# Attention's meta-value product as one fp32r product over 128 stacked rows, and the halo queries' output as one product

## The chip, the cores and the metric

The kernel runs on one core of one Trainium2 chip. The metric is the device time of one execution in microseconds, median of three runs: 1804.35 us before (1803.9 to 1806.26). A profile comes from one further execution, which took 1806.76 us itself; its span from the first to the last instruction is 1805.0 us.

## The reference, cut to what matters

Two hybrid blocks run one after the other over 512 tokens of width 1024. The first has an SSD branch, a sliding-window attention branch and a feed-forward part; the second has other mixers. The change touches only the attention of the first block. There, 16 query heads share two key/value heads of width 64. Every query of a block of 128 tokens sees the previous and its own block, and beside them 16 meta tokens that stand ahead of the sequence; a sink value joins the softmax.

```
s = concat(s_meta, s_band, sink)          # 16 + 256 + 1 columns per query
p = softmax(s)
p_meta = p[..., :16];  p_band = p[..., 16:-1]
out = einsum(p_meta, v_meta) + einsum(p_band, v_band)
```

The first of the two products of the last line, `p_meta` with `v_meta`, is what the change is about. All of it is fp32.

## The kernel before, in words

Activations lie with channels on the 128 partitions and tokens along the free axis. A weight matrix is loaded in tiles of 128x1024 (`wload`, line 67), and each tile is cut into a high part in fp32r (ScalarE copy, line 76) and the low rest (VectorE subtraction, line 77). A projection (`gemm`, lines 88 to 90) then makes three fp32r products for each 128x128 weight: high with high, high with low, low with high. A product whose operands are plain fp32 runs as two passes in the profile (two LDWEIGHTS and two MATMUL records for each call).

Attention (line 508) works on pairs of heads: `j` runs from 0 to 7, and in each pair the head of the first key/value head lies on partitions 0 to 63 and that of the second on 64 to 127. Its setup makes `kh` and `kl` (keys, high and low), `vtok` (values with tokens on the partitions), and `vm`: the 16 meta values of both key/value heads as a block-diagonal matrix of 32 rows and 128 columns (transpose at line 550, copy at line 551). Two halo queries ahead of the sequence see only meta tokens; lines 554 to 583 make their softmax and their output, the latter by eight small products of `vm` with two columns of `pth` each (line 581).

`scores(j)` (line 585) makes the scores of pair `j`, adds the bias, and takes the softmax in `s`. `values(j, s)` (line 627) makes the output:

```
pm = psum(g)                                            # four transposes: 32 meta columns x 512 queries (L633)
nc.vector.tensor_copy(ptm, pm[:32, :])                  # L634
pv = psum(g, "o")
nc.tensor.matmul(pv, vm, ptm, start=True, stop=False)   # L637
```

Then, for each of four query blocks, the band columns of `s` are transposed (lines 646 and 650), copied by ScalarE to `pt` (647, 651) and multiplied with `vtok` (656, 657) into the same accumulation `pv`. The product at line 637 opens this accumulation, so the 14 products (28 passes) of lines 656 and 657 of a pair stand behind it. ScalarE copies `pv` back over the queries (658).

The loop calls `scores(j + 1)` ahead of `values(j)`, and after each pair `fill` (line 226) adds two or three gate or branch projections (`gate_tile`, line 669, and `branch`, line 470), which are plain `gemm` work. PSUM has three buffers with the tag "g" (projections), two "a" (scores), two "t" (transposes; `pm` and the halo's are of these) and one "o" (`pv`).

The order in which each engine gets its instructions is not that of the program text. A planner goes over the whole program with priorities in the order of the text (weight loads come ahead, `high_priority`), simulates the engines with its own costs, and writes down a fixed order for every engine. In the trace, transposes, scores, projections and value products of several steps alternate on TensorE. An engine then executes its order strictly, waiting where it must.

When the attention's tiles are released, the tiles `ah` and `al` (line 58 and 59 of `split_hl`) take their place: the attention output cut into high and low parts, on which the next projection works. So the last pair's output stands ahead of everything that follows.

Of the kernel before, what the change touches and what calls it, by code (L numbers as in the profile page):

```python
# [12 lines left out]
F32 = mybir.dt.float32  # L13
F32R = mybir.dt.float32r
# [3 lines left out]
AF = mybir.ActivationFunctionType  # L18
ALU = mybir.AluOpType
# [96 lines left out]
def psum(g, tag="t"):  # L116
    return g.pp.tile([128, 512], F32, name=f"ps_{tag}", tag=tag, bufs=g.psb[tag])
# [90 lines left out]
LINE = 64  # L208
# [9 lines left out]
class Mixer:  # L218
# [289 lines left out]
    def attention(self, wk, nfill):  # L508
        g, nc = self.g, self.nc
# [18 lines left out]
        for k in range(2):  # L528
            r, z = half[k], half[1 - k]
# [18 lines left out]
        vm = wk.tile([32, 128], F32, name="vm", tag="vm")  # L548
        px = psum(g)
        nc.tensor.transpose(px[:32, :128], vbd, g.ident)  # L550
        nc.scalar.activation(vm, px[:32, :128], AF.Copy)
        sink = g.par[:, _BP["sink"]:_BP["sink"] + 16]

        hb = wk.tile([2, 256], F32, name="hb", tag="hb")
        nc.sync.dma_start(out=hb, in_=g.a["bias_h"])
        ph = psum(g)
# [17 lines left out]
        ph = psum(g)  # L574
        for j in range(8):
            nc.tensor.transpose(ph[:32, j * 2:j * 2 + 2], sh[:, j * 32:(j + 1) * 32], g.ident[:2, :2])
        pth = wk.tile([32, 16], F32, name="pth", tag="pth")
        nc.vector.tensor_copy(pth, ph[:32, :16])
        ph = psum(g)
        for j in range(8):  # L580
            nc.tensor.matmul(ph[:, j * 2:j * 2 + 2], vm, pth[:, j * 2:j * 2 + 2], start=True, stop=True)
        halo = wk.tile([128, 16], F32, name="halo", tag="halo")
        nc.vector.tensor_copy(halo, ph[:, :16])

# [41 lines left out]

        def values(j, s):
            q = qs[j]
            ptm = wk.tile([32, 512], F32, name="ptm", tag="ptm", bufs=2)
            pm = psum(g)  # L630
            for b in range(4):
                m0 = 256 if b else 128
                nc.tensor.transpose(pm[:32, b * 128:(b + 1) * 128], s[:, b, m0:m0 + 32], g.ident)  # L633
            nc.vector.tensor_copy(ptm, pm[:32, :])  # L634

            pv = psum(g, "o")
            nc.tensor.matmul(pv, vm, ptm, start=True, stop=False)  # L637
            for b in range(4):
                pt = wk.tile([128, 2, 2, 128], F32, name="pt", tag="pt", bufs=3)
                ptf = pt.rearrange("p a b c -> p (a b c)")  # L640
                px = psum(g)
                if b:
                    for k in range(2):
                        for t in range(2):
                            c0 = k * 288 + t * 128
                            nc.tensor.transpose(px[:, (k * 2 + t) * 128:(k * 2 + t + 1) * 128], s[:, b, c0:c0 + 128], g.ident)  # L646
                    nc.scalar.activation(ptf, px, AF.Copy)
                else:
                    for k in range(2):
                        nc.tensor.transpose(px[:, k * 128:(k + 1) * 128], s[:, 0, k * 160:k * 160 + 128], g.ident)  # L650
                    nc.scalar.activation(pt[:, :, 1, :], px[:, :256].rearrange("p (a c) -> p a c", a=2), AF.Copy)
                cols = slice(b * 128, (b + 1) * 128)
                for k in range(2):
                    rows = slice(k * 64, k * 64 + 64)
                    if b:
                        nc.tensor.matmul(pv[rows, cols], vtok[:, b - 1, rows], pt[:, k, 0, :], start=False, stop=False)
                    nc.tensor.matmul(pv[rows, cols], vtok[:, b, rows], pt[:, k, 1, :], start=False, stop=(b == 3))
            nc.scalar.activation(q[:, 2:NO], pv, AF.Copy)
            nc.vector.tensor_copy(q[:, 0:2], halo[:, 2 * j:2 * j + 2])

        prev = scores(0)
        for j in range(8):
            nxt = scores(j + 1) if j < 7 else None
            values(j, prev)
            prev = nxt
            self.fill(nfill[j])
# [905 lines left out]
```

## Time and profile before

| | before |
|---|---|
| median of 3 runs | 1804.35 us |
| profiled execution | 1806.76 us |
| its span | 1805.0 us |
| TensorE busy (matmul) | 1761.6 us, 98% |
| VectorE busy | 1135.6 us, 63% |
| ScalarE busy | 753.4 us, 42% |
| GpSimd busy | 296.2 us, 16% |
| mean granted TensorE clock | 0.992 |

"Busy" of TensorE counts from a pass's start to its modelled end, and passes overlap; so the share alone does not tell how much could be saved, and the distance between the starts of two passes is the better measure of what one costs. Line numbers (L637) are those of the kernel before; a line of a helper stands for all its callers, and the tile names tell them apart.

### The profile page before, as it was taken

To read this page: it belongs to the slowest core of one execution; us is meant where nothing else is said; L and a number is where in the kernel's file an instruction comes from. 1 tells how busy PE (TensorE), PEld (TensorE's weight loads), DVE (VectorE), ACT (ScalarE), POOL (GpSimd) and SP (SyncE) were. 2 spreads that over 40 slices of the span, in tenths; PEclk is the share of its full clock that TensorE was granted. 3 is DMA by queue.
4 is the path that set the end of the run, shared out by engine and by line. 5 is a ranking of instruction groups with operands and counts; after the bars stand their busy time and mean duration, and the time that the engine had idled before them with its cause. 6 is when DMAs were issued, how large, how long until landed. Compare 5 with 4: busy or idle time off the path is not lost.

```text
span 1805.0 us, 29863 instructions
## 1 busy us (share of the span) xinstructions
PE 1761.6 (98%) x12108; PEld 1590.8 (88%) x12108; DVE 1135.6 (63%) x2151; ACT 753.4 (42%) x1334; POOL 296.2 (16%) x287
## 2 busy tenths in 40 slices
PE   8999999999999999999999999999999999999997
PEld 8999999999889889999999988878888777878887
DVE  7797787855586755466677533577665676743543
ACT  4544444432336553334444433564443345632233
POOL 1254444533330002200000011100000000000112
PEclk9999999999999999999999999999999999999999
DMA  4223222222222222222222222221222121222222
GB/s 153 98 90 106 88 96 83 95 94 95 87 75 76 75 94 94 94 82 95 94 94 92 91 97 96 83 91 62 82 71 91 65 72 43 87 84 93 94 94 71
DMA packets 51341, 158.60 MB, mean 88 GB/s; under 512 B 5826, under 2 KB 9668, under 8 KB 51204
## 3 DMA queue, kind: packets, MB, share of 16 engines
q1 hardware_dynamic: 49348, 154.18, 25.0%
q10 hardware_dynamic: 1808, 2.39, 0.4%
q8 instruction: 95, 1.56, 0.3%
q14 instruction: 42, 0.34, 0.1%
q0 software_dynamic: 48, 0.13, 0.0%
HBM read 152.93 MB, written 2.16 MB: 86 GB/s over the span
## 4 chain that ended last, share of the span: by engine, by line
PE 85%; DVE 7%; ACT 3%; issue 2%; DMA 1%; POOL 1%; SPq 0%; DVEq 0%; ACTq 0%; POOLq 0%
PE ps_g L88 22%; PE ps_g L89 21%; PE ps_g L90 21%; PE ps_g L814 2%; PE ps_g L815 2%; PE ps_g L813 2%; DVE wlo L77 1%; DVE cv L340 1%; DMA E<-csd 1%; PE ps_o L1221 1%; POOL xe L394 1%; PE ps_t L646 1%; PE ps_a L957 1%; PE ps_t L413 1%; PE ps_a L444 1%
## 5 line engine op out<-in xcount | busy, mean ns | idle before, releaser
L76 ACT ACTIVATE whi<-wraw 128x1024 fp32r<-128x1024 f32 (+3 forms) x264 | 273.8, 1038 | 555.3 <-PE ps_g L89 336.6
L77 DVE TENSOR_TENSOR wlo<-wraw,whi 128x1024 fp32r<-128x1024 f32 (+3 forms) x264 | 339.9, 1288 | 142.6 <-ACT whi L76 141.8
L88 PE MATMUL ps_g<-uh,whi 128*128 128x256 f32 (+2 forms) x1056 | 303.8, 288 | 2.4 <-DVE z L186 1.4
L90 PE MATMUL ps_g<-uh,wlo 128*128 128x256 f32 (+2 forms) x1056 | 301.8, 286 | 0.0
L89 PE MATMUL ps_g<-ul,whi 128*128 128x256 f32 (+2 forms) x1056 | 301.1, 285 | 0.0
L88 PEld LDWEIGHTS ps_g<-uh,whi 128*128 128x128 f32 x1056 | 199.4, 189 | 4.5 <-DVE z L186 1.6
L88 PE MATMUL ps_g<-fh,whi 128*128 128x256 f32 (+1 forms) x704 | 199.1, 283 | 0.8 <-DVE fx L186 0.8
L89 PEld LDWEIGHTS ps_g<-ul,whi 128*128 128x128 f32 x1056 | 199.4, 189 | 0.5 <-issue 0.2
L90 PEld LDWEIGHTS ps_g<-uh,wlo 128*128 128x128 f32 x1056 | 199.4, 189 | 0.4 <-issue 0.3
L89 PE MATMUL ps_g<-fl,whi 128*128 128x258 f32 (+1 forms) x704 | 199.6, 284 | 0.0
L90 PE MATMUL ps_g<-fh,wlo 128*128 128x258 f32 (+1 forms) x704 | 198.5, 282 | 0.0
L88 PE MATMUL ps_g<-vh,whi 128*128 128x512 f32 x456 | 181.8, 399 | 2.3 <-DVE lf L846 1.8
L89 PE MATMUL ps_g<-vl,whi 128*128 128x512 f32 x456 | 181.8, 399 | 0.0
L90 PE MATMUL ps_g<-vh,wlo 128*128 128x512 f32 x456 | 181.4, 398 | 0.3 <-DVE wlo L77 0.3
L159 POOL TENSOR_TENSOR sq<-sq 128x514 f32<-128x514 f32 (+2 forms) x48 | 62.0, 1301 | 496.4 <-ACT sq L151 496.4
L88 PEld LDWEIGHTS ps_g<-fh,whi 128*128 128x128 f32 x704 | 133.8, 190 | 1.0 <-DVE fx L186 1.0
L89 PEld LDWEIGHTS ps_g<-fl,whi 128*128 128x128 f32 x704 | 134.1, 190 | 0.0
L90 PEld LDWEIGHTS ps_g<-fh,wlo 128*128 128x128 f32 x704 | 133.6, 190 | 0.0
L88 PEld LDWEIGHTS ps_g<-vh,whi 128*128 128x128 f32 x456 | 85.8, 188 | 20.9 <-ACT whi L76 2.2
L89 PEld LDWEIGHTS ps_g<-vl,whi 128*128 128x128 f32 x456 | 85.9, 188 | 18.5
L90 PEld LDWEIGHTS ps_g<-vh,wlo 128*128 128x128 f32 x456 | 85.8, 188 | 18.5 <-DVE wlo L77 0.8
L88 PE MATMUL ps_g<-yh,whi 128*128 128x256 f32 (+1 forms) x256 | 75.3, 294 | 1.5 <-DVE bt L481 1.1
(445 smaller groups left out, 3843.6 us busy)
## 6 DMA issues: line engine op xcount, KB each, us to landing
wraw<-in_w_in SPq DMA_DIRECT2D x128, 512.0 KB, 3.2
wraw<-in_w_ffn_in SPq DMA_DIRECT2D x44, 512.0 KB, 3.2
E<-csd SPq DMA_DIRECT2D x32, 265.0 KB, 3.9
wraw<-in_w_ssd SPq DMA_DIRECT2D x16, 512.0 KB, 3.3
wraw<-in_w_out SPq DMA_DIRECT2D x16, 512.0 KB, 3.3
wraw<-in_w_ffn_out SPq DMA_DIRECT2D x16, 512.0 KB, 3.2
wraw<-in_w_pab SPq DMA_DIRECT2D x16, 512.0 KB, 3.2
wraw<-in_w_att SPq DMA_DIRECT2D x8, 512.0 KB, 3.2
```

What stands on the lines that cost most here:

```text
L76: nc.scalar.activation(hf[:, :n], raw[:, :n], AF.Copy)
L77: (eng or nc.vector).tensor_tensor(lf[:, :n], raw[:, :n], hf[:, :n].bitcast(F32), ALU.subtract)
L88: nc.tensor.matmul(ps, wh, a, start=(i == 0), stop=False)
L89: nc.tensor.matmul(ps, wh, b, start=False, stop=False)
L90: nc.tensor.matmul(ps, wl, a, start=False, stop=(i == last))
L159: self.g.nc.gpsimd.tensor_tensor(a[:, :self.ntok], a[:, :self.ntok], sq[:, :self.ntok], ALU.add)
L340: nc.vector.scalar_tensor_tensor(cv, xr[:, j:j + NT], w(j), cv, ALU.mult, ALU.add)
L394: nc.gpsimd.tensor_tensor(xe[:CH].rearrange("p c (h d) -> p c h d", h=2), xd[:CH, 0:4, :].rearrange("p c (h d) -> p c h d", h=2), dtx(0, 4 ...
L413: nc.tensor.matmul(px[:, c * 128:(c + 1) * 128], bt[:CH, c, :], xe[:CH, c, :], start=True, stop=True)
L813: nc.tensor.matmul(ps, wh, uh, start=(k == 0), stop=False)
L814: nc.tensor.matmul(ps, wh, ul, start=False, stop=False)
L815: nc.tensor.matmul(ps, wl, uh, start=False, stop=(k == NFF - 1))
```

## The change

Three edits, all in `attention`.

1. In the setup, `vm4` is made beside `vm`: a 128x128 tile in fp32r whose rows 0 to 31 and 32 to 63 are the high part of `vm` (two ScalarE copies) and whose rows 64 to 95 and 96 to 127 are the low part (two VectorE subtractions).
2. The eight halo products of 2 columns become one of 16 columns.
3. In `values`, `ptm` becomes a 128x512 tile in fp32r: rows 0 to 31 high part (ScalarE copy out of PSUM), 32 to 63 low part (VectorE subtraction, PSUM and SBUF in), 64 to 127 a copy of rows 0 to 63 (VectorE). The product of `vm` and `ptm`, fp32 over 32 rows, becomes one of `vm4` and `ptm`, fp32r over 128 rows: the sum over the rows is high*high + high*low + low*high + low*low.

```
+        vm4 = wk.tile([128, 128], F32R, name="vm4", tag="vm4")
+        for r in (0, 32):
+            nc.scalar.activation(vm4[r:r + 32, :], vm, AF.Copy)
+        for r in (64, 96):
+            nc.vector.tensor_tensor(vm4[r:r + 32, :], vm, vm4[0:32, :].bitcast(F32), ALU.subtract)
...
-        for j in range(8):
-            nc.tensor.matmul(ph[:, j * 2:j * 2 + 2], vm, pth[:, j * 2:j * 2 + 2], start=True, stop=True)
+        nc.tensor.matmul(ph[:, :16], vm, pth, start=True, stop=True)
...
-            ptm = wk.tile([32, 512], F32, name="ptm", tag="ptm", bufs=2)
+            ptm = wk.tile([128, 512], F32R, name="ptm", tag="ptm", bufs=2, align_bytes=LINE)
...
-            nc.vector.tensor_copy(ptm, pm[:32, :])
+            nc.scalar.activation(ptm[0:32, :], pm[:32, :], AF.Copy)
+            nc.vector.tensor_tensor(ptm[32:64, :], pm[:32, :], ptm[0:32, :].bitcast(F32), ALU.subtract)
+            nc.vector.tensor_copy(ptm[64:128, :], ptm[0:64, :].bitcast(F32))
...
-            nc.tensor.matmul(pv, vm, ptm, start=True, stop=False)
+            nc.tensor.matmul(pv, vm4, ptm, start=True, stop=False)
```

## Rows read from the trace of the kernel before

**Rows 1.** The page: busy time of each engine over the span, and the chain of work that ended last, by engine.

```profile
PE 1761.6 (98%) x12108; PEld 1590.8 (88%) x12108; DVE 1135.6 (63%) x2151; ACT 753.4 (42%) x1334; POOL 296.2 (16%) x287
PE 85%; DVE 7%; ACT 3%; issue 2%; DMA 1%; POOL 1%; SPq 0%; DVEq 0%; ACTq 0%; POOLq 0%
```

**Rows 2.** Busy time by stretch, over the attention stage and its two ends. Columns: stretch in us, its length, busy time (and number of instructions) of TensorE, its weight loads, VectorE, ScalarE and GpSimd, granted TensorE clock, DMA share, GB/s. The last row takes the stage as one.

```profile
505.00:530.00 25.00, 23.56 (x205) 22.82 (x205) 21.99 (x66) 9.38 (x25) 12.43 (x7) 0.97 0.20 67
530.00:555.00 25.00, 25.00 (x210) 23.24 (x210) 19.75 (x60) 13.27 (x32) 2.24 (x2) 1.00 0.26 83
555.00:580.00 25.00, 25.00 (x208) 21.60 (x206) 15.89 (x46) 13.54 (x35) 0.00 (x0) 1.00 0.25 84
580.00:605.00 25.00, 25.00 (x207) 22.35 (x206) 15.86 (x51) 16.09 (x46) 0.00 (x0) 1.00 0.23 73
605.00:630.00 25.00, 25.00 (x210) 22.91 (x209) 19.04 (x59) 12.88 (x32) 0.00 (x0) 1.00 0.23 75
630.00:655.00 25.00, 25.00 (x206) 21.32 (x205) 12.19 (x43) 16.15 (x47) 0.00 (x0) 1.00 0.12 43
655.00:680.00 25.00, 23.51 (x199) 20.89 (x198) 14.07 (x25) 12.07 (x20) 1.62 (x2) 1.00 0.40 135
505.00:680.00 175.00, 172.07 (x1432) 155.14 (x1432) 118.79 (x345) 93.37 (x232) 16.30 (x10) 1.00 0.24 80
```

**Rows 3.** The chain that ended last, in order of time, between 490 and 700 us. Columns: start, time it held the chain, what. The eight pieces of line 637 lie between the two shown and are all 1.05 us long.

```profile
502.59 1.02 ACT kh L531
503.63 1.15 DVE kl L532
504.80 0.65 DVE kh L533
...
521.99 1.87 PE ps_t L581 x16
...
538.09 1.05 PE ps_o L637 x2
...
661.12 1.05 PE ps_o L637 x2
```

**Rows 4.** TensorE's timeline around the first meta-value product. Columns: start, duration, engine, line, operation, tiles, shape, count.

```profile
537.68 0.29 PE L88 MATMUL ps_g<-uh,whi 128*128 128x256 f32 x1
537.81 0.28 PE L89 MATMUL ps_g<-ul,whi 128*128 128x256 f32 x1
538.02 1.12 PE L637 MATMUL ps_o<-ptm,vm 32*128 32x512 f32 x2
539.07 0.43 PE L657 MATMUL ps_o<-pt,vtok 128*64 128x128 f32 x2
539.43 0.39 PE L608 MATMUL ps_a<-kh,qx 128*128 128x272 f32 x1
539.66 0.28 PE L609 MATMUL ps_a<-kl,qx 128*128 128x272 f32 x1
539.88 0.32 PE L657 MATMUL ps_o<-pt,vtok 128*64 128x128 f32 x1
```

**Rows 5.** The timeline in a later stage, where fp32r products of 128 rows by 512 columns follow each other.

```profile
1100.09 0.39 PE L813 MATMUL ps_g<-aH,whi 128*128 128x512 f32 x1
1100.32 0.40 PE L814 MATMUL ps_g<-aL,whi 128*128 128x512 f32 x1
```

**Rows 6.** The timeline of VectorE at the copies that feed the product of line 637, for the first, fourth and last of the eight pairs, and TensorE's at the fourth and last product.

```profile
535.46 0.67 DVE L634 COPY ptm<-ps_t 32x512 f32<-32x512 f32 x1
...
590.29 0.68 DVE L634 COPY ptm<-ps_t 32x512 f32<-32x512 f32 x1
594.22 1.12 PE L637 MATMUL ps_o<-ptm,vm 32*128 32x512 f32 x2
...
659.42 0.68 DVE L634 COPY ptm<-ps_t 32x512 f32<-32x512 f32 x1 [1.41 <-PE ps_t L633]
661.05 1.12 PE L637 MATMUL ps_o<-ptm,vm 32*128 32x512 f32 x2
```

**Rows 7.** Groups of instructions by line and shape between 480 and 690 us: operation, tiles, shape, count, busy us, mean ns of one, idle time of its engine just before them. They are the operations of the stage nearest to those that the change adds.

```profile
L647 ACT ACTIVATE pt<-ps_t 128x512 f32<-128x512 f32 x24 | 13.9, 590 | 22.6 <-PE ps_t L646 22.6
L551 ACT ACTIVATE vm<-ps_t 32x128 f32<-32x128 f32 x1 | 0.3, 267 | 1.7 <-PE ps_t L550 1.7
L600 DVE TENSOR_TENSOR qx<-q,qx 64x512 fp32r<-64x512 f32 x16 | 11.0, 686 | 0.6 <-ACT qx L599 0.2
L573 DVE TENSOR_TENSOR sh<-sh,rh 2x256 f32<-2x256 f32 x1 | 0.4, 408 | 0.0
L567 DVE TENSOR_TENSOR eh<-par,mh 2x16 f32<-2x16 f32 x1 | 1.2, 1250 | 0.0
```

**Rows 8.** The timeline: a second copy of line 533, which ran while GpSimd worked.

```profile
506.06 2.20 POOL L484 TENSOR_TENSOR acc<-acc,bt 128x514 f32<-128x514 f32 x1 [14.92 <-DVE bt L481]
507.11 1.66 DVE L533 CAST kh<-kh 64x960 fp32r<-64x960 f32 x1
```

**Rows 9.** Waits of TensorE between 505 and 690 us: who waited for whom, us in total, times, longest.

```profile
PE ps_a L608 <- DVE mx L610: 1.4, 1, 1.4
PE ps_g L88 <- ACT ah L58: 1.2, 1, 1.2
PE ps_o L656 <- ACT pt L647: 0.2, 1, 0.2
```

## The prediction, written before the changed kernel was run

> **What bounds the kernel now.** I read the page first. TensorE is busy for 1761.6 us of the span and holds 85% of the chain that ended last; VectorE holds 7% and ScalarE 3% of it [rows 1]. For an edit inside one stage that average is not enough, so next came the busy time by stretch over the attention. From 530 to 655 us TensorE is busy in every microsecond, at a granted clock of 1.00, while VectorE has 12 to 20 and ScalarE 13 to 16 of each 25 us, and GpSimd almost nothing. The two ends are different: from 505 to 530 TensorE has 23.56 and VectorE 21.99 of 25, and from 655 to 680 TensorE has 23.51 [rows 2]. So in the middle TensorE alone sets the pace, at the start VectorE is nearly as tight, and at the end something leaves TensorE idle for 1.5 us. The list of its waits names both holes: 1.4 us for a score bias on VectorE (L610), 1.2 us for the cut attention output on ScalarE (`ah`), and 0.2 us for `pt` [rows 9]. Then the chain itself: the meta-value product stands in it eight times with 1.05 us, and the halo products once with 1.87 us [rows 3]. What is taken from these is taken from the path.
>
> **The change part by part.** I sum against the profiled execution, 1806.76 us (its span is 1805.0; 1.76 lie around it), and carry the difference over to the median, 1804.35, which is 2.4 us lower.
>
> *The product of line 637.* It runs as two passes, and from the start of the first to the start of what follows on TensorE lie 1.05 us [rows 4]. Its successor is one fp32r pass over 128 rows and 512 columns; such passes follow each other every 0.23 us [rows 5]. Each pair gains 1.05 - 0.23 = 0.82, eight pairs 6.56 us. The bounds come from the passes around it. A plain 128x128 product has 0.13 us to its successor; the step from 128x128 to another form has 0.21 (L89 to L637) and 0.22 (L609 to L657), about 0.09 more [rows 4]. If the new product saves such a step at its entry, a pair gains 0.91; if it pays one more at its exit, 0.73. That makes 5.8 to 7.3 us; I take 6.56, which lies between and is what the chain's own pieces say.
>
> A rule speaks against this term. The Trainium skill, page "Perfetto Trace Analysis", section "Engine Utilization", halves the array's rate for what it calls FP32_LOW_HIGH; if that is this two-pass form, it should cost two fp32r passes, 0.46 us, and the gain would be 0.23 a pair. The trace shows 1.05 in each of the eight [rows 3], 4.6 times the fp32r pass, nearer to the four passes of "FP8 and Floating Point Precision", section "TensorE Precision Notes".
>
> *The halo products.* Sixteen passes of two columns hold the chain for 1.87 us [rows 3], 0.117 each. Two passes of 16 columns are left. The columns are not what a pass of 2 costs, so I leave the price of a pass as it is: 14 x 0.117 = 1.64 us gone. Bounds: 1.4 if a pass of 16 columns costs twice one of two, 1.87 if the rest hides.
>
> *The setup of `vm4`.* Two ScalarE copies of 32x128 cost 0.27 each, as L551 [rows 7]; ScalarE has 9.38 of 25 us of work there [rows 2], so they cost nothing unless that cover goes, then 0.54. The two subtractions go to VectorE, which is nearly full there and for which TensorE waited 1.4 us [rows 2, 9]. 256 columns take 0.41 (L573) and 512 take 0.69 (L600), so 128 columns take about 0.27 [rows 7]. They come ahead of the scores in the text, so the planner may put them ahead of the first L610. I charge both to the path, 0.54. Bounds: nothing where they fall into VectorE's idle 3 us; 2.5 if both run as slowly as L567, 1.25 us for 16 columns [rows 7].
>
> *Making `ptm`.* One VectorE copy of 0.68 becomes three steps. The ScalarE copy out of PSUM is like L647, 0.59; the subtraction like L600, 0.69 [rows 7]; the copy of 64x512 like L533, 0.65 for 960 columns, so 0.35 for 512 [rows 3]. The same three steps in a row on the keys (L531, L532, L533) show a hand-over of 0.02 us between engines [rows 3]. The new chain is 1.67 long, 0.99 more than the old. That is hidden if the product was late anyway: it starts 1.89 us after its copy ended in the first pair (536.13 to 538.02), 3.25 in the fourth and 0.95 in the last [rows 4, 6], the largest and the smallest of the eight being among these. Seven pairs have room for it on the old order, and the last misses by 0.04. What hides it is projection work on TensorE; without cover it would be 8 x 0.99 = 7.9 us. Busy time: VectorE gets 8 x 0.36 = 2.9 us and ScalarE 8 x 0.59 = 4.7 us on 118.79 and 93.37 of 175 [rows 2], so neither becomes the bound. Queues: behind the subtraction, waiting for ScalarE, stand evictions of scores and projections, which free PSUM; behind the product stand the 28 passes of its accumulation and the projections. The planner writes a new order in which the product may stand later. I charge 0.2 us in all; bounds 0 and 7.9, nearest to the 0.04 of the last pair.
>
> A slow copy is possible: the second L533 took 1.66 us while GpSimd worked, 0.89 for 512 columns [rows 8]. GpSimd is idle from 555 to 655 [rows 2], so this can touch the first pair only.
>
> *Sum.* -6.56 - 1.64 + 0.54 + 0.2 = -7.5 us: 1799.3 for a profiled execution, **1796.9 on the median**. The shorter TensorE work moves the rest ahead as a whole; nothing late in the attention waits for a DMA in rows 9.
>
> **The rivals.** 0.2% is 3.6 us, about what can be told from no change here.
>
> *A. The sum above*, 1794.9 to 1799.9, chance 0.60. For it: a TensorE without a gap from 530 to 655.
>
> *B. Part of it is lost to the longer `ptm` chain.* The product comes 0.5 us late in every pair, because the new ScalarE copy stands behind an exponential and the subtraction behind a weight subtraction. -7.5 + 8 x 0.5 = -3.5: 1800.9. For it: in-order queues 50 to 80% full. Against it: slack of 0.95 to 3.25. Chance 0.19.
>
> *C. Slower: the opener becomes the bound.* `pm` holds one of two transpose buffers until the subtraction, one ScalarE copy longer, and `pv` is the only buffer of its kind; if the product opens late, the transposes and the 28 passes behind it stand still and the projections put between them run out. The price is the wait w of each pair: it eats the gain at w = 7.5/8 = 0.94 us and is slower by 3.6 us at 1.39. With w = 1.5 the time is 1804.35 - 7.5 + 12 = 1808.9. For it: the new chain has three queues where there was one. Against it: 0.99 of lengthening alone does not reach it; the planner would have to misjudge the queues in nearly every pair. Chance 0.08.
>
> *D. Nothing to see.* The new order costs at the stage's ends what the middle gains: VectorE at the start up to 2.5 us, the tail, which nothing covers, up to 1.6, ill-placed projections the rest; the time is 1803 to 1805. Chance 0.09.
>
> *E. The rate of the fp32 form is not what changes.* By the half-rate rule, the rest of the 1.05 us being a wait that stays, the gain is 8 x 0.23 = 1.84, and with the other terms -1.84 - 1.64 + 0.74 = -2.7: 1801.6. Against it: eight equal pieces of 1.05 us, which a wait would not give. Chance 0.04. Last of all, a product with fp32r operands might still run in two passes; I give that no chance of its own, since every fp32r product here is one.
>
> **How the numbers follow.** Faster by over 0.2% (below 1800.7): all of A and half of B, with a little of D and C for a better order than I see: 0.72. Within 0.2%: the rest of B, most of D, E: 0.19. Slower: C and the worst of D: 0.09. The range must hold 8 in 10: from 1792.5, where both cuts take their upper bound (7.3 + 1.87) and the new order is 2.7 us kinder than the old, to 1803.5, which takes in B and E and leaves out C and most of D.
>
> **What would show each step.** In the changed profile, the meta-value product is eight single passes over 128 rows, with about 0.23 us to the next start; the halo is two passes within 0.25 us. TensorE stays full in the middle, and the stage from the first score to the first product with `ah` is 7 to 8 us shorter. The copies of `ptm` show 0.59, 0.69 and 0.35 us, and the last of them ends ahead of its product. B and C would show as waits of the product for VectorE in the list of TensorE's waits, C also as transposes waiting for a buffer; D as longer holes at 505 to 530 or at the end. The prediction is wrong if the stage shrinks by less than 4 us, or if it shrinks and another stage grows.

## The result, and the profile after

The changed kernel takes 1796.44 us (median of 6 runs, 1794.09 to 1798.49), beside 1805.55 us for the kernel before in the same comparison: a ratio of 0.9944 with a 95% interval of 0.9934 to 0.9954, or 10.1 us (8.3 to 11.9). Timed once more, unaltered, it gave 1796.69 us and 0.9941 (0.9927 to 0.9955). The forecast was 1796.9 us, 7.5 less than before: sign and size hold, the gain is somewhat larger than the sum. That the median lies within 0.5 us of the forecast is luck: the kernel before took 1.2 us more here than in the three runs from which the forecast started. The ratio of e8 below leaves out two of its eleven runs, of 2133 and 2904 us, whose mean granted clock was 0.75 and 0.61.

The page of the changed kernel, whose profiled execution took 1794.09 us: busy time of each engine, and the chain that ended last by engine.

```profile
PE 1748.9 (98%) x12086; PEld 1585.4 (88%) x12086; DVE 1141.2 (64%) x2161; ACT 759.3 (42%) x1344; POOL 298.7 (17%) x287
PE 86%; DVE 7%; ACT 3%; issue 2%; POOL 1%; DMA 1%; DVEq 0%; SPq 0%; ACTq 0%; POOLq 0%
```

Beside [rows 1], TensorE has 22 passes fewer (14 at the halo, 8 second passes) and 12.7 us less work; VectorE has 5.6 us more and ScalarE 6.0. The bound has not moved. Where the time was saved shows when the span is cut in three: up to the transpose of `vbd` in line 550, from there to the first product with `ah` (called the stage from here on), and the rest. First the kernel before, busy time by stretch, with the columns of [rows 2]:

```profile
0.00:508.40 508.40, 487.80 (x4112) 475.93 (x4112) 369.62 (x656) 212.38 (x323) 201.25 (x212) 0.99 0.28 98
508.40:666.90 158.50, 155.73 (x1303) 139.02 (x1300) 106.74 (x328) 85.94 (x222) 12.47 (x7) 1.00 0.23 76
666.90:1805.00 1138.10, 1118.08 (x6696) 975.83 (x6696) 659.25 (x1168) 455.05 (x790) 82.43 (x68) 0.99 0.25 85
```

The same three stretches of the changed kernel, and the first 25 us of the attention:

```profile
0.00:506.80 506.80, 486.03 (x4111) 474.55 (x4112) 370.56 (x658) 212.56 (x323) 202.31 (x213) 0.99 0.29 98
506.80:654.40 147.60, 145.41 (x1282) 135.67 (x1280) 112.47 (x337) 91.16 (x232) 13.07 (x7) 1.00 0.24 78
654.40:1792.30 1137.90, 1117.48 (x6696) 975.14 (x6696) 658.18 (x1168) 455.62 (x790) 83.28 (x68) 0.99 0.25 86
...
505.00:530.00 25.00, 24.25 (x204) 23.08 (x204) 24.60 (x71) 9.78 (x27) 11.61 (x7) 0.98 0.27 87
```

The part behind is the same to 0.2 us, the stage is 10.9 us shorter, and the part ahead, which the change does not touch, differs by 1.6. That first part moves between executions: it ends anywhere from 505.9 to 510.6 us in the profiles of this study, at 509.1 in the second one of the changed kernel, whose stage is 148.8 us long with 145.35 of TensorE work. So a single span is a poor ruler here. TensorE's busy time in the stage is a good one as long as the granted clock stays at 1.00 there, as in these rows: the two profiles of the same kernel agree to 0.06 us, and between the kernels it falls by 10.3. That is the number to account for.

The chain of waits of the changed kernel (start, time held, what): the halo, the first product of line 645, which was line 637, and the end of the attention.

```profile
520.90 0.32 PE ps_t L587 x2
...
537.56 0.23 PE ps_o L645
...
653.69 0.63 ACT ah L58
```

Seven of the eight products stand in the chain, with 0.23 or 0.24 us each, against 1.05 in [rows 3]; the halo holds 0.32 against 1.87. The instructions on `ptm` in the changed kernel (shortest, median and longest in ns, first and last start, shapes):

```profile
L640 ACT ACTIVATE ptm<-ps_t x8: 572/588/591, 532.5 to 647.5; 32x512 fp32r<-32x512 f32 x8
L641 DVE TENSOR_TENSOR ptm<-ps_t,ptm x8: 679/680/681, 534.3 to 648.1; 32x512 fp32r<-32x512 f32 x8
L642 DVE CAST ptm<-ptm x8: 412/421/422, 535.6 to 648.8; 64x512 fp32r<-64x512 f32 x8
L645 PE MATMUL ps_o<-ptm,vm x8: 391/476/482, 537.3 to 649.7; 128*128 128x512 f32 x8
```

TensorE's waits in the attention of the changed kernel, as in [rows 9]:

```profile
PE ps_g L88 <- ACT ah L58: 1.2, 1, 1.2
PE ps_a L614 <- DVE mx L616: 0.7, 2, 0.5
PE ps_o L664 <- ACT pt L655: 0.2, 1, 0.2
```

No product waits for `ptm`. The wait for `mx` fell from 1.4 to 0.7 here, but it is 2.0 in the second profile of the same kernel, so its size says nothing of the change.

### The profile page after: what moved, and what is told of

It is laid out like the page before. It is cut to its first block, busy times and chain, and to the rows that moved or that the text cites. A ratio compares the mean times of both kernels' runs of the same rounds, so it can differ in the third digit from the quotient of the medians.

```text
span 1792.3 us, 29852 instructions
## 1 busy us (share of the span) xinstructions
PE 1748.9 (98%) x12086; PEld 1585.4 (88%) x12086; DVE 1141.2 (64%) x2161; ACT 759.3 (42%) x1344; POOL 298.7 (17%) x287
## 4 chain that ended last, share of the span: by engine, by line
PE 86%; DVE 7%; ACT 3%; issue 2%; POOL 1%; DMA 1%; DVEq 0%; SPq 0%; ACTq 0%; POOLq 0%
PE ps_g L88 22%; PE ps_g L89 22%; PE ps_g L90 22%; PE ps_g L822 2%; PE ps_g L823 2%; PE ps_g L821 2%; DVE wlo L77 1%; DVE cv L340 1%; PE ps_o L1229 1%; POOL xe L394 1%; DMA E<-csd 1%; PE ps_t L413 1%; PE ps_a L965 1%; PE ps_a L444 1%; PE ps_t L654 1%
```

## The experiments

A word used below: a *group* is a stretch of band products (the 128*64 form, lines 656 and 657 before, 664 and 665 after) with no other form of matmul between them, counted in each kernel's list of TensorE instructions. The planner writes a new list for each kernel; the instructions of the parts not edited are the same in all.

| run | edit | ratio (95%) | stage, us | TensorE busy in it | groups |
|---|---|---|---|---|---|
| before | | 1 | 158.5 | 155.73 | 30 |
| after | | 0.9944 (0.9934 to 0.9954) | 147.6 | 145.41 | 23 |
| e1 | halo only | 0.9984 (0.9975 to 0.9993) | 155.9 | 152.60 | 28 |
| e2 | product only | 0.9976 (0.9965 to 0.9986) | 152.6 | 149.12 | 27 |
| e3 | product in fp32 | 0.9957 (0.9944 to 0.9970) | 153.1 | 151.12 | 25 |
| e4 | 32 high rows only | 0.9959 (0.9945 to 0.9973) | 151.3 | 150.07 | 34 |
| e5 | product twice | 0.9959 (0.9946 to 0.9971) | 151.9 | 148.64 | 24 |
| e9 | before, meta part last | 0.9961 (0.9947 to 0.9974) | 152.3 | 148.28 | 8 |
| e8 | after, meta part last | 0.9987 (0.9978 to 0.9997) | 156.3 | 145.51 | 8 |
| e11 | before, last in 7 pairs | 0.9966 (0.9954 to 0.9978) | 150.4 | 148.75 | 10 |
| e10 | after, last in 7 pairs | 0.9968 (0.9958 to 0.9978) | 150.5 | 143.87 | 8 |
| e12 | e10, product in fp32 | 1.0008 (1.0000 to 1.0017) | 158.5 | 149.40 | 9 |
| e13 | after, again | 0.9941 (0.9927 to 0.9955) | 148.8 | 145.35 | 23 |
| e14 | after, last in pairs 2 to 4 | 0.9942 (0.9929 to 0.9954) | 147.4 | 143.34 | 16 |

**Each half alone.** e1 is the kernel before with one halo product:

```
-        for j in range(8):
-            nc.tensor.matmul(ph[:, j * 2:j * 2 + 2], vm, pth[:, j * 2:j * 2 + 2], start=True, stop=True)
+        nc.tensor.matmul(ph[:, :16], vm, pth, start=True, stop=True)
```

> Only the halo products become one; the meta-value product stays fp32 over 32 rows. Theory 'passes' (the gain is TensorE's own time, term by term): the halo pieces fall from 1.88 to 0.31 us, so 1.6 us faster, and its order has 28 groups of band products (lines 656, 657) instead of 30, about 0.2 us each, so 2.0 us in all: ratio 0.9989. Theory 'order' (most of the gain comes from the planner's new order, which any edit stirs up): no relation to the 1.6 us, anything from 3 us slower to 5 us faster.

e2 is the changed kernel with these lines the other way round, the eight halo products kept.

> Only the meta-value product changes; the halo stays eight products. Theory 'passes': the product's pieces fall from 8.4 to 3.1 us, and 27 groups of band products instead of 30 give 0.6 more: 5.9 us faster, ratio 0.9967; together with the halo-only kernel the two add up to about 8, near the 9 of the whole change. Theory 'order': the two parts do not add up to the whole, one of them alone gives 0 to 3 us or all 9.

e1 is faster by 2.9 us (0.0016 of 1806.15), its stage by 2.6; the halo holds the chain for 0.32 us there too. e2 is faster by 4.3 us and its stage by 5.9. The stages add to 8.5 of the 10.9 us, the times to 7.2 of 10.1. Part of what is missing stands in e2's busy time by stretch:

```profile
524.00:526.00 2.00, 2.00 (x18) 1.98 (x18) 1.97 (x7) 1.95 (x8) 1.05 (x1) 1.00 0.56 139
526.00:528.00 2.00, 2.00 (x12) 2.00 (x11) 1.97 (x10) 2.00 (x9) 1.15 (x1) 0.50 0.47 150
528.00:530.00 2.00, 2.00 (x13) 2.00 (x13) 1.97 (x11) 0.52 (x3) 0.82 (x1) 0.65 0.59 191
```

The granted clock is at its lower level (0.50, 1.2 of 2.4 GHz) for some 3.4 us while TensorE is full; the passes of those 3.4 us would take 1.7 at the upper one. e5 has such a stretch near 512 us. The other runs of e2 have lost time in this way too: the mean granted clock of its eight runs is 0.9899, that of the kernel before in the same comparison 0.9923. A mean that is lower by 0.0024 over 1800 us stands for some 8.6 us more at the lower level, an estimate, and so for some 4.3 us lost while TensorE is full; where in the span is not on record. That is more than the 2.9 us that are missing from the sum of the two times, so this sum says little about whether the halves add up. The runs of e5 show no such difference (0.9918 beside 0.9920).

**What the product's new price is made of.** Three variants of the changed kernel, each with one edit. e3 takes the same 128 rows in fp32:

```
-            nc.tensor.matmul(pv, vm4, ptm, start=True, stop=False)
+            nc.tensor.matmul(pv, vm4.bitcast(F32), ptm.bitcast(F32), start=True, stop=False)
```

> The whole change, but the product over the 128 stacked rows is told to run as fp32 (the same bytes read as fp32), so in two passes. Theory 'passes': the product costs about 1.05 us a pair again, the making of the stacked tile costs nothing, the halo gives 1.6 and 25 groups instead of 30 give 1.0: 2 to 3 us faster than before, ratio 0.9985. Theory 'order' or 'stacking': as fast as the whole change, ratio 0.9944. If the making of the stacked tile costs what its added 0.99 us a pair could at most, it is 5 us slower than before.

e4 keeps fp32r and takes 32 rows. It leaves out the low parts of `vm` and `ptm`, with the instructions that make and stack them, and so three of the four partial sums (`vm4` is cut in the same way, to one ScalarE copy):

```
-            ptm = wk.tile([128, 512], F32R, name="ptm", tag="ptm", bufs=2, align_bytes=LINE)
+            ptm = wk.tile([32, 512], F32R, name="ptm", tag="ptm", bufs=2, align_bytes=LINE)
...
-            nc.scalar.activation(ptm[0:32, :], pm[:32, :], AF.Copy)
-            nc.vector.tensor_tensor(ptm[32:64, :], pm[:32, :], ptm[0:32, :].bitcast(F32), ALU.subtract)
-            nc.vector.tensor_copy(ptm[64:128, :], ptm[0:64, :].bitcast(F32))
+            nc.scalar.activation(ptm, pm[:32, :], AF.Copy)
```

> The low parts are left out: the stacked tile is only the 32 rows of the high part (one ScalarE copy, no VectorE step), and the product is one fp32r pass over 32 rows; the output lacks the low parts of the meta product. Theory 'passes': the product gains as in the whole change, VectorE's two steps cost nothing there, but its order has 34 groups of band products instead of 23, so about 2.2 us slower than the whole change: 7 us faster than before, ratio 0.9961. If VectorE's two steps cost something in the whole change (1.1 us a pair at most), this one is faster than it: ratio 0.992 or less. If a product over 32 rows pays for a change of form on both sides, 8 x 0.1 us slower still: 0.9965.

e5 issues the product twice, so that the meta values are counted double:

```
-            nc.tensor.matmul(pv, vm4, ptm, start=True, stop=False)
+            for r in range(2):
+                nc.tensor.matmul(pv, vm4, ptm, start=(r == 0), stop=False)
```

> The whole change, with the product of each pair issued twice in a row into the same accumulation, so the meta part counts double in the output. It measures what one such pass costs on the path. Theory 'passes': 8 x 0.23 = 1.8 us slower than the whole change (24 groups of band products, one more: 0.2): ratio to before 0.9955. If the 0.41 us that a product holds in the changed kernel is the pass itself and not the step to the 64-column form behind it: 8 x 0.41 = 3.3 slower, ratio 0.9963.

The chain of waits gives each its price. In e3, first and last of eight equal pieces:

```profile
537.88 0.86 PE ps_o L645 x2
...
649.63 0.86 PE ps_o L645 x2
```

In e4, first and last of eight pieces of 0.42 or 0.43:

```profile
536.04 0.43 PE ps_o L640
...
650.88 0.42 PE ps_o L640
```

In e5, the first of eight, of which seven are 0.46 or 0.47:

```profile
540.39 0.47 PE ps_o L646 x2
```

With 1.05 of [rows 3] and 0.23 after, that fills a square: two fp32 passes cost 1.05 over 32 rows and 0.86 over 128, one fp32r pass 0.42 to 0.43 and 0.23, two of those 0.47. From fp32 to fp32r saves 0.62 to 0.63 in either form, from 32 rows to 128 saves 0.19 to 0.20 at either rate. Of the 0.82 a pair, the rate is three quarters (8 x 0.63 = 5.0 us) and the form of 32 rows the rest (8 x 0.19 = 1.5). So e4, with a quarter of the products and two VectorE steps less in each pair, has a *dearer* product, by 8 x 0.195 = 1.6 us of chain. Its stage is longer by 3.7 us, but most of that goes with its 11 groups more, to which the next experiment comes. Stacking to 128 rows is not a cost of the change; it is part of its gain.

The runs' times are less tidy than the pieces. e3 lies only 0.0013 above the changed kernel, 2.3 us, where its product costs 8 x 0.63 = 5.0 more, and its interval overlaps the other's; in its stage TensorE has 5.7 us more to do than in the changed kernel's, and the stage is 5.5 longer. In its profiled execution the part ahead ended at 505.9 us, the earliest of all; whether the rest of the difference lies there in the other runs is open.

**The order, with the instructions held fixed.** The busy times of e1 to e5 could not be explained by product and halo alone, but each list had another number of groups. e8 and e9 change only the text's order: the band transposes and the copies to `pt` of all four blocks come first, then the meta part, then the band products in one loop (`pt` gets a fourth buffer). e9 is the kernel before, e8 the changed one:

```
+            pts = []
             for b in range(4):
-                pt = wk.tile([128, 2, 2, 128], F32, name="pt", tag="pt", bufs=3)
+                pt = wk.tile([128, 2, 2, 128], F32, name="pt", tag="pt", bufs=4)
...
+                pts.append(pt)
...
+            for b, pt in enumerate(pts):
```

> The kernel before (fp32 product over 32 rows, eight halo products) with the same rearrangement: 8 groups of band products instead of 30, 44 changes of form instead of 131. Theory 'changes of form': 87 x 0.1 = 8.7 us less, up to 2 us back in the tail: ratio 0.9960. With orders this much alike, the distance to the rearranged changed kernel is the change alone: theory 'passes' 5.3 + 1.6 = 6.9 us, theory 'order' much less.

> The whole change, with the band's transposes and copies of a pair placed ahead of the meta part and the band products in a loop of their own (four buffers of pt). The same work; the planner's order then has 8 groups of band products instead of 23 and 42 changes of form on TensorE instead of 112. Theory 'the rest of the gain is fewer changes of form, about 0.1 us each': 70 x 0.1 = 7 us less on TensorE, less up to 2 us for a longer tail of the last pair: 5 to 7 us faster than the whole change, ratio 0.991. Theory 'it is something else in the order (a wait, the clock)': no faster than the whole change, and 1 to 2 us slower from the tail: 0.995.

e9 is as expected: the same instructions as before in another order, 22 groups fewer, 7.45 us less TensorE work, 7.0 us less time. The stage of e9, busy time by stretch:

```profile
509.70:662.00 152.30, 148.28 (x1304) 138.19 (x1302) 107.55 (x329) 86.74 (x222) 12.46 (x7) 1.00 0.26 82
```

e8 is a miss by some 14 us. Its waits of TensorE in the stage say why:

```profile
PE ps_t L644 <- DVE ptm L657: 3.1, 1, 3.1
PE ps_t L648 <- DVE s L630: 2.3, 1, 2.3
...
PE ps_o L661 <- DVE ptm L658: 1.9, 1, 1.9
```

There are the waits for `ptm` that the changed kernel does not have. They all fall at the stage's end, where no projection is left to put between: TensorE idles for 156.3 - 145.51 = 10.8 us of the stage, some 8 us more than in the changed kernel (2.2 and 3.5 in its two profiles). The rest of the miss is the clock, which falls in the hole:

```profile
650.00:652.00 2.00, 0.00 (x0) 0.00 (x0) 1.97 (x5) 0.75 (x2) 0.00 (x0) 0.93 0.00 0
...
654.00:656.00 2.00, 2.00 (x18) 1.79 (x19) 0.00 (x0) 0.47 (x2) 0.00 (x0) 0.50 1.00 361
...
662.00:664.00 2.00, 2.00 (x15) 1.56 (x17) 0.00 (x0) 0.00 (x0) 0.00 (x0) 0.50 0.00 0
```

So TensorE's work did not fall as its order promised: it is 145.51 us, where the line of the next section, with products and halo added, gives 140.3 for 8 groups. The other runs that the ratio counts have lost time in this way, too: their mean granted clock is 0.9891, beside 0.9920 of the kernel before in the same comparison, an estimated 5 us.

e10 and e11 try to keep the end covered: the last pair stays in the old sequence, the other seven take the new one. e12 is e10 with e3's line.

```
+            if j < 7:
+                pts = [turn(b) for b in range(4)]
+                pv = meta()
+                for b in range(4):
+                    band(b, pts[b], pv)
+            else:
+                pv = meta()
+                for b in range(4):
+                    band(b, turn(b), pv)
```

> The whole change with the band's transposes ahead of the meta part as in the meta-last kernel, but the last pair in the old sequence, so that its opener is not late. 8 groups of band products on TensorE instead of 23 in the changed kernel. From the stages of the nine profiles so far, a group costs TensorE about 0.34 us beside its products. Theory 'groups': 15 x 0.34 = 5 us less TensorE time in the stage than the changed kernel; what TensorE idles at the end comes on top (the meta-last kernel idled 10.8 us, of which about 7 at the end; the changed one 2.2). If the end is mended: 3 to 5 us faster than the changed kernel, ratio 0.992; if TensorE still runs out of projections there: 0.996.

> The kernel before with that same sequence (10 groups). The distance between this one and its changed twin is the change with nearly one order: theory 'passes' 5.3 for the product and 1.6 for the halo, with two groups 0.7: 7.6 us, ratio to before 0.9965 if the twin is at 0.992. Theory 'order': less than 4 us apart.

> The changed kernel's twin with the product over the 128 stacked rows as fp32, two passes (9 groups). Theory 'passes': the product holds 7.6 us instead of 3.1, so 4.5 us (with one group 4.8) slower than the twin with fp32r: 0.0026 in ratio. Theory 'order': the same as the twin.

e12 and e10 have the same text but for the product's type: 0.0040 of 1806.84, 7.2 us, of which 8 x 0.63 = 5.0 are the rate; the hole at the end of e12 is larger, too (9.1 us idle against 6.6). e10 and e11 missed the distance that I expected between them, and came out equal. The pieces are right: TensorE has 4.9 us less to do in e10. But less work means that e10 runs out of projections before its last pairs. First its waits, then its busy time by stretch:

```profile
PE ps_t L640 <- DVE s L630: 3.2, 4, 2.5
PE ps_t L661 <- DVE ptm L642: 1.5, 1, 1.5
```

```profile
644.00:646.00 2.00, 0.28 (x2) 0.11 (x2) 1.48 (x7) 2.00 (x5) 0.00 (x0) 1.00 0.00 0
646.00:648.00 2.00, 0.85 (x3) 0.27 (x3) 2.00 (x5) 1.46 (x3) 0.00 (x0) 0.80 0.00 0
648.00:650.00 2.00, 1.09 (x5) 0.78 (x6) 1.94 (x5) 0.05 (x1) 0.00 (x0) 0.50 0.38 100
650.00:652.00 2.00, 2.00 (x14) 1.56 (x15) 0.24 (x1) 0.21 (x1) 0.00 (x0) 0.50 1.00 361
652.00:654.00 2.00, 2.00 (x22) 1.89 (x18) 0.00 (x0) 0.77 (x2) 0.00 (x0) 0.50 0.17 64
654.00:656.00 2.00, 2.00 (x23) 1.60 (x21) 0.00 (x0) 1.69 (x3) 0.00 (x0) 0.99 0.00 0
```

The gain of the product is given back twice: TensorE idles for 6.6 us of the stage (e11: 1.65), and after the hole its clock stands at 0.50 for some six us, in which the 5.1 us of busy time from 648 to 654 would have been 2.5.

**The changed kernel again, and the new sequence in the middle alone.** e13 is the changed kernel again (its numbers are above); e14 takes the new sequence in three pairs of the middle alone, with a line of e10 changed:

```
-            if j < 7:
+            if j in (2, 3, 4):
```

> The changed kernel unaltered, timed again beside the next one. First timing: ratio 0.9944, interval 0.9934 to 0.9954. Expected the same; its stage without waits and without a lowered clock should again be about 145.4 us of TensorE work.

> The changed kernel with the band's transposes ahead of the meta part in pairs 2, 3 and 4 alone, so that the end keeps nearly the old sequence: 16 groups of band products instead of 23. Theory 'groups': 7 x 0.34 = 2.4 us less TensorE work in the stage, 143.0; of the last pair's transposes only 7 projection passes are left to cover, so 1 to 2 us of waiting come back: ratio 0.9938, half a microsecond to 1.5 faster than the changed kernel. If the end runs dry as in the meta-last kernels and the clock falls there: 0.996 or more.

The stage of e14, and its longest wait of TensorE:

```profile
508.20:655.60 147.40, 143.34 (x1282) 135.78 (x1279) 112.17 (x337) 90.75 (x232) 13.05 (x7) 1.00 0.26 83
```

```profile
PE ps_t L657 <- ACT pt L658: 2.0, 1, 2.0
```

Its TensorE work came out at 143.34 us, with 143.0 expected. Its time did not follow: a new wait of 2.0 us for `pt` takes the gain, and 0.9942 beside 0.9941 is no difference. No version here beats the changed kernel. Of the 10.7 us of e13's comparison an estimated 2 are the clock, whose mean is 0.9913 in the runs of the kernel before and 0.9924 in e13's; in the other three comparisons in which it is on record, the kernel before has 0.9920 to 0.9923.

## Why the prediction was right, and where it was short

*The sum that the runs give.* I take from the TensorE work of each stage the product by its piece of the chain, the halo (1.87 or 0.32) and, in e2 and e5, the 1.7 us lost at the lower clock. What is left is 145.46 us for the kernel before, 143.25 after, 143.88 in e1, 143.71 in e2, 143.92 in e3, 146.35 in e4, 142.90 in e5, 138.01 in e9, 138.48 in e11 and 141.18 in e14. A straight line over the groups, 135.6 + 0.32 x groups, meets all ten within 0.7 us. (e8, e10 and e12 are left out, since the clock falls in their holes.) So before to after: the product -8 x 0.82 = -6.56, the halo -1.55, seven groups -7 x 0.32 = -2.2; together -10.3, with 10.3 measured. e9 shows the third term by itself. The line is a fit, and the kernels before and after are among its points; but e10, e11 and e14 had a price of 0.34 a group on record before they ran. e14's work bears it out (143.34 with 143.0 expected), and e11's (148.75, where 155.73 - 20 x 0.34 is 148.9); in e10 the clock fell.

What carries the price is not settled. The changes of form of every kind fall together with the groups: counted in the stage's records, as forms of 128, 64 or 32 rows and columns, they are 133 before, 106 after, 46 in e9, 57 in e11 and 82 in e14. A line over them, 134.0 + 0.084 x changes, meets the same ten within 0.7 us, and gives the order 2.3 us (27 x 0.084) in place of 2.2. Between kernels that differ in the order alone, a change comes to 0.086 (e9), 0.092 (e11) and 0.086 us (e14), a group to 0.34, 0.35 and 0.30.

*The product*: right, -6.56 by the chain's pieces. The detail "0.23 us to the next start" is not what the starts show. TensorE's timeline around the first product of the changed kernel, whose predecessors are transposes, and around the second:

```profile
537.17 0.38 PE L654 MATMUL ps_t<-mats,s 128*128 128x128 f32 x2
537.31 0.47 PE L645 MATMUL ps_o<-ptm,vm 128*128 128x512 f32 x1
537.72 0.44 PE L665 MATMUL ps_o<-pt,vtok 128*64 128x128 f32 x4
537.99 0.44 PE L664 MATMUL ps_o<-pt,vtok 128*64 128x128 f32 x4
538.20 0.44 PE L665 MATMUL ps_o<-pt,vtok 128*64 128x128 f32 x4
538.57 0.44 PE L654 MATMUL ps_t<-mats,s 128*128 128x128 f32 x2
...
554.13 0.28 PE L90 MATMUL ps_g<-uh,wlo 128*128 128x256 f32 x1
554.25 0.40 PE L645 MATMUL ps_o<-ptm,vm 128*128 128x512 f32 x1
554.57 0.44 PE L665 MATMUL ps_o<-pt,vtok 128*64 128x128 f32 x4
```

At the second, from the projection ahead to the band product behind lie 0.12 + 0.32 us, where [rows 4] have 0.21 + 1.05: again 0.82. Both bounds came true at once, a step of 0.09 saved at the entry and one of 0.09 paid at the exit. Behind transposes, as at the first, the exit shows 0.41, and the entry less by as much (0.03 us from the start of the last transpose). Starts put a change of form on one neighbour, ends on the other; a sum must use one of the two throughout.

*The rate rule* (rival E) is refuted: with the rows and the form held fixed, the type alone takes e3's 0.86 us to 0.23. The half-rate rule of the Trainium skill ("Perfetto Trace Analysis", "Engine Utilization"), if its FP32_LOW_HIGH is this two-pass form, would make two fp32 passes cost two fp32r ones, 0.47 as e5 has them; e3 has 0.86. The forecast did not split its 0.82; 0.19 of it is the form of 32 rows.

*The halo*: 1.64 forecast, 1.55 by the chain. A pass of 16 columns costs 0.16 (0.32 / 2), less than twice one of two (0.117), as the bounds had it, but the two together are not within the 0.25 us that was named as the sign.

*The setup of `vm4`*: charged with 0.54, not seen. VectorE rose to 24.60 of the 25 us from 505 to 530, but TensorE has 24.25 there against 23.56 [rows 2], and in its work nothing is left over (the kernels before and after lie 0.3 us off the first line above, both). As a wait it would stand under `mx`: 0.7 and 2.0 us in the two profiles of the changed kernel, 1.4 before [rows 9]. A cost of 0.54 is neither seen there nor ruled out.

*The `ptm` chain*: charged with 0.2. Steps of 0.59, 0.68 and 0.42 us, the last forecast as 0.35, so VectorE has 0.42 in place of 0.35 there. The cover held: TensorE has no wait for `ptm`, in the last pair either, where VectorE's timeline shows

```profile
648.11 0.68 DVE L641 TENSOR_TENSOR ptm<-ps_t,ptm 32x512 fp32r<-32x512 f32 x1 [2.04 <-ACT ptm L640]
648.82 0.42 DVE L642 CAST ptm<-ptm 64x512 fp32r<-64x512 f32 x1
```

and the product starts at 649.74, 0.50 us after the copy ends. B and C did not come; e8 shows that C's mechanism exists, at the end of the stage, once the text's order takes the cover away.

*The order*: the step that was short. The forecast had no term for it and took it for a cost (D), with room for a kinder order in the range alone; it is worth -2.2 us here. [rows 4] had shown the price of one change of form, about 0.09, and the forecast used it at the product alone; how many changes the new list would have, it did not ask. Why the planner needs fewer groups for the changed kernel was not tried.

## What to carry to other kernels

Where one engine is the bound, price an edit by the pieces that it leaves in the chain, neighbours included, and then ask what it does to the order: changes of matmul form were worth more here than the halo products, and e9 gained 7 us without removing an instruction. Filling the array's rows with low parts can be cheaper than a product of few rows. And a stage that lives on filler work has an end: what is saved in its middle is worth something only while filler is left for its last steps (e8, e10).

## What the runs showed of the hardware that was not expected

- A product of 32 rows costs 0.19 to 0.20 us more than one of 128 rows, in fp32 and in fp32r (1.05 and 0.86; 0.42 and 0.23).
- Each group of band products costs some 0.32 us beyond its passes by the first line above, or each change of form 0.08 to 0.09 by the second. In the rows around 538 us it is read as 0.09 on the product ahead, 0.05 at the first four passes (0.27 against 0.22) and 0.15 at the last four (0.37, from 538.20 to 538.57), 0.29 together. The Trainium skill, "TensorEngine Tiling (Array Packing)", "Key Properties", says that a change of tiling mode drains TensorE; that these rows lose time at both ends of a group agrees with it. The same section of the Trainium skill lets different tiles work in parallel, and the trace agrees: four fp32 passes of 128 columns of the 64-column form take 0.22 us, half of what the columns of e3's product would need (0.86 / 2 / 4 = 0.11 each).
- TensorE's granted clock fell to 0.50 after a hole (0.28 of 2 us busy in e10, none of 2 us in e8) and came back after full stretches; in e2 it stood at 0.50 for some 3.4 us with TensorE full in the rows ahead of it. The rows do not say why.
